# A hybrid decoder layer on one core: input-projection weights in sets of 256 columns, and the embedding weights kept on chip

## The chip, the cores and the metric

The kernel runs on one core of a Trainium2 chip. The core has five engines with queues of their own: TensorE (PE, with its weight loads shown as PEld), VectorE (DVE), ScalarE (ACT), GpSimd (POOL) and SyncE (SP), which here issues most of the DMAs. The metric is the device time of one execution in microseconds (us). Three runs of the kernel before took 2463.92 to 2465.51 us, with a median of 2464.99.

## What is computed

The reference is one decoder layer over 2048 tokens of width 1024, cut here to the parts that matter:

```python
u = rmsnorm(h, ln1_g)
q, k, v, g, g_lr, cb, cc, cx = split(u @ w_in)        # 256, 256, 512, 512, 16, 512, 512, 512 columns
log_a = log_sigmoid(g_lr @ w_gate_up + b_gate) / 16
o = gla_chunked(q / 8, k, v, log_a)                   # gated linear attention, 4 heads
o = rmsnorm(o, gn_g) * silu(g)
y = cb * causal_depthwise_conv(cc * cx, conv_w)
h = h + concat(o, y) @ w_out
a, b = split(rmsnorm(h, ln2_g) @ w_gate_upffn)        # 2 x 2816 columns
h = h + (silu(a) * b) @ w_down
gate = sigmoid(rmsnorm(h, ln3_g) @ w_ple_gate)
h = h + gate * (p @ w_ple_proj)                       # p: 2048 x 256 embeddings
return rmsnorm(h, lnf_g)
```

All data are float32.

## The kernel before

**Products.** Each float32 operand is split into a high part (the operand cast to fp32r) and a low part (the rest), by one cast on ScalarE and one subtraction on VectorE (`split`, lines 103 to 107, or `split_into`, line 161). `product` (line 144) multiplies, for each k of 128 rows, high by high, high by low and low by high: three matmuls per k. A `unit` (line 153) is such a product over the eight k of the width 1024, 24 matmuls of 128x512, followed by the eviction of its PSUM bank and by ticks. A tick advances delayed work and one step of the gated attention, which is written as a generator (`gla`, line 360) and so is interleaved with the units.

**Three phases.** The mixing phase does input projection, attention, convolution and output projection for four blocks of 512 tokens; at its end it turns the embeddings `p` of the first 1024 tokens and multiplies them by `w_ple_proj`. The up phase starts with the same product for the other 1024 tokens, and then multiplies by `w_gate_upffn` in seven products per group (a Strassen scheme, in the order 1, 6, 2, 5, 7, 3, 4), with operands U that the mixing phase has written to DRAM. The last phase does `w_down`, the gate and the final norm.

**Order of the queues.** In the mixing phase only PE's order is the program's; the other engines' queues are ordered at compile time by a scheduler. In the up and last phases all five queues follow the program. A queue runs strictly in its order, so an instruction that waits holds up all behind it.

**The input projection in a block** (`mixing`). First come v and the low-rank gate (528 columns). Then come five weight sets of 512 columns: `wq` (q and k), two `wc` (256 columns of cc with 256 of cx each), `wg` and `wb`. A set is loaded by `weights` (line 109) in four `raw` tiles of two k each, with rows of 2 KB (1 KB where the set has two segments), and split into eight `hl` tiles, one per k, each with 512 high and 512 low values per partition. Four units then read all eight tiles, each unit its own 128 columns. There are eleven `hl` buffers and four `raw` buffers, used in rotation. The weights are the stationary operand, the activations (`uT`) the moving one. The attention's generator starts with the first unit on `wq`; it puts chains on ScalarE, VectorE and GpSimd (`Abs`, `Exp`, `Ln`, a scan at line 378, then `level_elementwise`, lines 389 to 403).

**The embeddings.** `embedding_turned` (line 712) turns `p` on PE and, at the first call, loads and splits `w_ple_proj` into four `hl` tiles. `embedding` (line 719) multiplies. In the up phase (from line 862) `p` is loaded to two of the three `ur` buffers, `w_ple_proj` is loaded again to two `raw` buffers and split into a buffer of the pool `U2` (`wpp`), and `p` is turned and split into another (`p_turned`). Then come 16 units of six matmuls (u = 0 to 15). Between them, `events` fetch and cut the first operands U of the gate product: each fetch is two DMAs of 512 KB to `ur` buffers, each cut two casts and two subtractions. The operands of the first four products go to the pool `uT` (four buffers of 16 KB per partition, shared by both phases), the other three to `U2` (three buffers).

Of the kernel before, what the change touches and what calls it, by code (L numbers as in the profile page):

```python
# [8 lines left out]
F32 = mybir.dt.float32  # L9
# [5 lines left out]
P = 128  # L15
# [24 lines left out]
def hybrid_layer(ctx: ExitStack, tc: tile.TileContext,  # L40
# [68 lines left out]
    def weights(src, segs, k0=0, nk=NK, between=None):  # L109
        width = sum(n for _, n in segs)  # L110
        tiles = []
        for k in range(k0, k0 + nk, 2):
            raw = load_pair(src, k, width, segs)
            if between:
                between(k)
            for i in range(2):
                tiles.append(split(raw[:, i, :], width))
        return lambda k, s: tiles[k][:, s, :]

# [148 lines left out]
            split_into(dst(0, sl), dst(1, sl), tp)  # L270

    U = [{}, {}]

    def fetch_U(b, n, gate=None):

# [20 lines left out]
    def mixing_phase(st):  # L296
# [251 lines left out]
        def mixing(b, u1, first):  # L548

            vt = [w4([P, 2, 512]) for _ in range(2)]  # L550
            wv = weights(w_in, [(O_V, 512), (O_LR, 16)], between=first)

            def v_done(ps, ti, n):
                dst = vt[ti // 2][:, ti % 2, :]
                if n == 0:
                    nc.scalar.copy(out=dst[:, 0:264], in_=ps[:, 0:264])
                    return
                lr = tiny.tile([P, 16], F32, name="lr")
                nc.vector.tensor_copy(out=lr, in_=ps[:, 248:264])
                nc.scalar.copy(out=dst[:, 264:512], in_=ps[:, 0:248])  # L560

                def low_rank():
                    tp = tr_bank()
                    nc.tensor.transpose(out=tp[0:16, 0:P], in_=lr, identity=ident)
                    nc.vector.tensor_copy(out=lrT[0:16, ti * P:(ti + 1) * P], in_=tp[0:16, 0:P])
                later(2, low_rank)

            for ti in range(NT):
                if first is not None:
                    first(8 + ti)  # L570
                cols = [slice(n * 264, (n + 1) * 264) for n in range(2)]
                banks = [mm_bank() for _ in range(2)]
                lhs = uT_at(u1, tok_of(ti))
                if first is not None and ti == 0:
                    for k in range(NK):
                        for n in range(2):
                            for i, (a, c) in enumerate(PASSES):
                                nc.tensor.matmul(out=banks[n][:, 0:264], lhsT=lhs(k, a), rhs=wv(k, c)[:, cols[n]],
                                                 start=(k == 0 and i == 0), stop=(k == NK - 1 and i == 2))
                    v_done(banks[0], ti, 0)  # L580
                    v_done(banks[1], ti, 1)
                    continue
                for n in range(2):
                    unit(banks[n][:, 0:264], lhs, lambda k, s: wv(k, s)[:, cols[n]], NK,
                         lambda: v_done(banks[n], ti, n))
            mix = [None, None]
            wq = weights(w_in, [(O_Q, 512)])
            qT = w4([P, 2, T])
            kT = w4([P, 2, T])
            gsT = [w4([P, 2, T]) for _ in range(2)]  # L590
            side[0] = gla(qT, kT, vt, gsT, mix)
            for j in range(4):
                ps = mm_bank()

                def qk_done():
                    if j < 2:
                        nc.scalar.mul(out=qT[:, j, :], in_=ps, mul=0.125)
                    else:
                        nc.scalar.copy(out=kT[:, j - 2, :], in_=ps)
                unit(ps, lambda k, s: wq(k, s)[:, j * P:(j + 1) * P], uT_at(u1, full), NK, qk_done)  # L600

            mix[1] = big([P, 4, 2, T], F32R)
            yt = [w4([P, 2, T]) for _ in range(2)]
            for g in range(2):
                wc = weights(w_in, [(O_CC + g * 256, 256), (O_CX + g * 256, 256)])
                for jj in range(2):
                    j = g * 2 + jj
                    z = t2([P, T + 2])
                    pc = mm_bank()

                    def cc_done():
                        nc.gpsimd.tensor_copy(out=z[:, 0:2], in_=halo[:, j, :])
                        nc.scalar.copy(out=z[:, 2:T + 2], in_=pc)
                    unit(pc, lambda k, s: wc(k, s)[:, jj * P:(jj + 1) * P], uT_at(u1, full), NK, cc_done)
                    px = mm_bank()

                    def cx_done():
                        nc.vector.tensor_tensor(out=z[:, 2:T + 2], in0=px, in1=z[:, 2:T + 2], op=ALU.mult)
                        nc.gpsimd.tensor_copy(out=halo[:, j, :], in_=z[:, T:T + 2])
                        y = yt[g][:, jj, :]  # L620
                        nc.vector.tensor_scalar(out=y, in0=z[:, 2:T + 2], scalar1=cw[:, 2, j:j + 1], scalar2=None,
                                                op0=ALU.mult)
                        nc.vector.scalar_tensor_tensor(out=y, in0=z[:, 1:T + 1], scalar=cw[:, 1, j:j + 1], in1=y,
                                                       op0=ALU.mult, op1=ALU.add)
                        nc.vector.scalar_tensor_tensor(out=y, in0=z[:, 0:T], scalar=cw[:, 0, j:j + 1], in1=y,
                                                       op0=ALU.mult, op1=ALU.add)
                    unit(px, lambda k, s: wc(k, s)[:, 256 + jj * P:256 + (jj + 1) * P], uT_at(u1, full), NK, cx_done)
            wg = weights(w_in, [(O_G, 512)])
            for h in range(4):
                ps = mm_bank()  # L630

                def g_done():
                    gs = t2([P, T])
                    nc.scalar.activation(out=gs, in_=ps, func=AF.Silu)
                    nc.vector.tensor_scalar(out=gsT[h // 2][:, h % 2, :], in0=gs, scalar1=gng, scalar2=None, op0=ALU.mult)
                unit(ps, lambda k, s: wg(k, s)[:, h * P:(h + 1) * P], uT_at(u1, full), NK, g_done)

            wb = weights(w_in, [(O_CB, 512)])
            for j in range(4):
                ps = mm_bank()  # L640

                def cb_done():
                    y = yt[j // 2][:, j % 2, :]
                    last["cb"] = nc.vector.tensor_tensor(out=y, in0=ps, in1=y, op=ALU.mult)
                    split_into(mix[1][:, j, 0, :], mix[1][:, j, 1, :], y)
                unit(ps, lambda k, s: wb(k, s)[:, j * P:(j + 1) * P], uT_at(u1, full), NK, cb_done)
            while side[0] is not None:
                tick()
            return mix
# [62 lines left out]
        def embedding_turned(q):  # L712
# [1 line left out]
                emb0["pT"] = big([P, 4, 2, T], F32R)  # L714
            turned_p(emb0["p"][q], lambda s, sl: emb0["pT"][:, 2 * q:2 * q + 2, s, sl], tr_bank)
            if q == 0:
                emb0["w"] = [weights(w_pp, [(n * 512, 512)], 0, 2) for n in range(2)]

        def embedding():
            for ti in range(EQ * NT):  # L720
                o = w4([P, D])
                for n in range(2):
                    ps = mm_bank()
                    product(ps, lambda k, s: emb0["pT"][:, 2 * (ti // NT) + k, s, tok_of(ti % NT)], emb0["w"][n], 2)
                    nc.scalar.copy(out=o[:, n * 512:(n + 1) * 512], in_=ps)
                    tick()
                nc.gpsimd.dma_start(out=emb[ti], in_=o)
# [39 lines left out]
    def up_phase(st):  # L767
# [95 lines left out]
        for q in range(EQ, NB):  # L863
            pts.append(pl["ur"].tile([P, 2, T], F32, name="ur"))
            nc.sync.dma_start(out=pts[-1].rearrange("p a t -> p (a t)").rearrange("p (t d) -> p t d", t=NT),
                              in_=p[q * T:(q + 1) * T, :].rearrange("(t p) d -> p t d", p=P))
        wpp_raw = [raw().rearrange("p q n -> p (q n)").rearrange("p (k n) -> p k n", k=2) for _ in range(2)]
        for n in range(2):
            nc.sync.dma_start(out=wpp_raw[n], in_=w_pp[:, n * 512:(n + 1) * 512].rearrange("(k p) n -> p k n", p=P))
        p_turned, wpp = [pl["U2"].tile([P, 4, 2, T], F32R, name="U2") for _ in range(2)]  # L870
        for n in range(2):
            split_into(wpp[:, 2 * n:2 * n + 2, 0, :], wpp[:, 2 * n:2 * n + 2, 1, :], wpp_raw[n])

        def pT(q):
            return lambda k, s: p_turned[:, (q - EQ) * 2 + k, s, :]
        for q in range(EQ, NB):
            o = (q - EQ) * 2
            turned_p(pts[q - EQ].rearrange("p a t -> p (a t)").rearrange("p (t d) -> p t d", t=NT),
                     lambda s, sl: p_turned[:, o:o + 2, s, sl], mm_bank)
        cuts = []  # L880

        def fetch_next(j):
# [2 lines left out]
        def cut_all():  # L885
            while cuts:
                cuts.pop(0)()
        events = {0: lambda: (fetch_next(0), run(-6), run(-5), run(-4)), 3: lambda: (cut_all(), fetch_next(1)),
                  6: lambda: (cut_all(), fetch_next(2), run(-3)), 9: lambda: (cut_all(), fetch_next(3), run(-2)),
                  12: lambda: (cut_all(), fetch_next(4)), 13: lambda: run(-1)}  # L890
        stores = []
        u = 0
        for q in range(EQ, NB):
# [530 lines left out]
```

## Time and profile before

| what | value |
|---|---|
| median of three runs | 2464.99 us |
| the profiled execution | 2461.07 us |
| its span, first to last instruction | 2459.4 us |
| PE busy | 2373.1 us, 96% |
| DVE, ACT, POOL busy | 57%, 40%, 29% |
| mean granted clock of PE | 0.990 |
| mixing phase | about 0 to 947 us |
| up phase | about 947 to 1843 us |

In the page and its views, an engine's idle time stands before the instruction that ended it, with the one that released it behind an arrow (`<-`). `L148` is line 148 of the kernel; as helpers record the operations, one line serves many tiles, and the tiles' names tell them apart: `mm<-uT,hl` is the input projection from its second set on, `mm<-hl,uT` v, the output projection and the first embeddings' product, `mm<-U,U` the second phase's embeddings' product, `U<-raw` the split of `wpp`, `U<-mm` that of the turned `p`, `uT<-ur` and `U<-ur` the cuts of U. Matmuls overlap each other, so that one of 128x512 lasts about 390 ns in the records while a stream of them advances by about 224 ns each.

### The profile page before, as it was taken

To read this page: it belongs to the slowest core of one execution; us is meant where nothing else is said; L and a number is where in the kernel's file an instruction comes from. 1 tells how busy PE (TensorE), PEld (TensorE's weight loads), DVE (VectorE), ACT (ScalarE), POOL (GpSimd) and SP (SyncE) were. 2 spreads that over 40 slices of the span, in tenths; PEclk is the share of its full clock that TensorE was granted. 3 is DMA by queue.
4 is the path that set the end of the run, shared out by engine and by line. 5 is a ranking of instruction groups with operands and counts; after the bars stand their busy time and mean duration, and the time that the engine had idled before them with its cause. 6 is when DMAs were issued, how large, how long until landed. Compare 5 with 4: busy or idle time off the path is not lost. (4 is left out here: it accounts for less than half of the span.)

```text
span 2459.4 us, 31386 instructions
## 1 busy us (share of the span) xinstructions
PE 2373.1 (96%) x11752; PEld 1941.7 (79%) x11752; DVE 1397.8 (57%) x1676; ACT 975.6 (40%) x1533; POOL 705.7 (29%) x604
## 2 busy tenths in 40 slices
PE   7999999999999997999999999999999999999995
PEld 6777878777887786788888888888887888788774
DVE  4665475556646652655555655445546556655777
ACT  4434433453445334422222432222224344435556
POOL 3301210431103015334334244244532105301522
PEclk9999999999999998999999999999999999999998
DMA  4226322831442259735445675567757668866997
GB/s 156 69 69 202 109 85 102 247 110 57 170 158 69 69 175 293 280 135 185 150 155 171 208 270 202 193 216 255 257 204 288 201 226 282 284 194 227 322 330 287
DMA packets 274761, 471.08 MB, mean 192 GB/s; under 512 B 22688, under 2 KB 146096, under 8 KB 274608
## 3 DMA queue, kind: packets, MB, share of 16 engines
q1 hardware_dynamic: 272112, 460.66, 55.5%
q0 software_dynamic: 2496, 8.41, 1.4%
q8 instruction: 92, 1.51, 0.2%
q14 instruction: 61, 0.50, 0.1%
HBM read 326.92 MB, written 142.08 MB: 191 GB/s over the span
## 5 line engine op out<-in xcount | busy, mean ns | idle before, releaser
L1069 PE MATMUL ps<-wh,mh 128*128 128x512 f32 x2496 | 579.4, 393 | 11.7 <-ACT mh L162 6.3
L1069 PEld LDWEIGHTS ps<-wh,mh 128*128 128x128 f32 x2496 | 469.7, 189 | 115.1 <-ACT mh L162 9.1
L148 PE MATMUL mm<-uT,hl 128*128 128x512 f32 x1920 | 479.0, 403 | 9.8 <-DVE hl L106 6.0
L148 PE MATMUL mm<-uT,wu 128*128 128x512 f32 x2112 | 482.3, 389 | 0.0
L148 PEld LDWEIGHTS mm<-uT,wu 128*128 128x128 f32 x2112 | 396.6, 188 | 82.1
L148 PEld LDWEIGHTS mm<-uT,hl 128*128 128x128 f32 x1920 | 354.9, 189 | 103.6 <-DVE hl L106 11.4
L148 PE MATMUL mm<-U,wu 128*128 128x512 f32 x1584 | 362.9, 389 | 2.1 <-DVE v L218 2.1
L148 PEld LDWEIGHTS mm<-U,wu 128*128 128x128 f32 x1584 | 297.4, 188 | 64.0 <-issue 2.5
L163 DVE TENSOR_TENSOR wu<-raw,wu 128x1024 fp32r<-128x1024 f32 x154 | 221.7, 1440 | 205.8 <-ACT wu L162 205.8
L148 PE MATMUL mm<-hl,uT 128*128 128x512 f32 (+1 forms) x1584 | 299.1, 348 | 3.4 <-DVE uT L163 2.1
L148 PEld LDWEIGHTS mm<-hl,uT 128*128 128x128 f32 x1584 | 250.5, 189 | 42.7 <-DVE uT L163 2.7
L162 ACT CAST wu<-raw 128x1024 fp32r<-128x1024 f32 x154 | 161.4, 1049 | 302.6 <-PE mm L148 220.4
L163 DVE TENSOR_TENSOR wh<-wr,wh 128x1024 fp32r<-128x1024 f32 x111 | 141.2, 1272 | 219.9 <-ACT wh L162 219.5
L218 DVE TENSOR_TENSOR v<-mm,v 128x512 f32<-128x512 f32 x220 | 150.9, 687 | 149.8 <-PE mm L148 149.0
L218 POOL TENSOR_TENSOR v<-v,v 128x512 f32<-128x512 f32 x88 | 137.9, 1567 | 300.2 <-DMA hid<-v 234.3
L162 ACT CAST wh<-wr 128x1024 fp32r<-128x1024 f32 x111 | 110.8, 998 | 253.3 <-PE ps L1069 200.7
L106 DVE TENSOR_TENSOR hl<-raw,hl 128x512 fp32r<-128x512 f32 (+1 forms) x260 | 183.7, 744 | 27.5 <-ACT hl L105 27.2
L105 ACT CAST hl<-raw 128x512 fp32r<-128x512 f32 (+1 forms) x260 | 153.9, 623 | 62.7 <-PE mm L148 33.2
L218 POOL TENSOR_TENSOR raw<-raw 128x1024 f32<-128x1024 f32 x44 | 107.2, 2446 | 217.7 <-issue 154.7
L163 DVE TENSOR_TENSOR mh<-mr,mh 128x1024 fp32r<-128x1024 f32 x111 | 143.8, 1296 | 8.9 <-ACT mh L162 8.6
L162 ACT CAST mh<-mr 128x1024 fp32r<-128x1024 f32 x111 | 110.6, 997 | 12.7 <-DMA mr<-hid 7.7
L218 POOL TENSOR_TENSOR ur<-ur 128x512 f32<-128x512 f32 x60 | 95.2, 1587 | 32.0 <-DMA ur<-in_w_ple_gate_dram 26.9
(190 smaller groups left out, 1884.4 us busy)
## 6 DMA issues: line engine op xcount, KB each, us to landing
raw<-in_w_gate_upffn_dram SPq DMA_DIRECT2D x77, 512.0 KB, 4.5
hid<-v SPq DMA_DIRECT2D x154, 256.0 KB, 3.6
mr<-hid SPq DMA_DIRECT2D x70, 512.0 KB, 4.6
raw<-in_w_in_dram SPq DMA_DIRECT2D x64, 512.0 KB, 4.5
wu<-raw SPq DMA_DIRECT2D x44, 512.0 KB, 2.9
raw<-wu SPq DMA_DIRECT2D x44, 512.0 KB, 5.8
wr<-wd SPq DMA_DIRECT2D x40, 512.0 KB, 3.7
w<-in_x_dram SPq DMA_DIRECT2D x32, 512.0 KB, 8.9
```

Source lines behind the costliest of these rows:

```text
L105: nc.scalar.copy(out=hl[:, 0, :], in_=raw)
L106: nc.vector.tensor_tensor(out=hl[:, 1, :], in0=raw, in1=hl[:, 0, :].bitcast(F32), op=ALU.subtract)
L148: nc.tensor.matmul(out=out_ap, lhsT=lhs(k, a), rhs=rhs(k, b), start=(start and k == 0 and i == 0), stop=(k == nk - 1 and i == 2), **kw)
L162: nc.scalar.copy(out=hi, in_=src)
L163: nc.vector.tensor_tensor(out=lo, in0=src, in1=hi.bitcast(F32), op=ALU.subtract)
L218: return e.tensor_tensor(out=out, in0=a, in1=b, op=op)
L1069: nc.tensor.matmul(out=bk[n][t], lhsT=M[a][:, j, tok_of(t)], rhs=W[c][:, j, :], start=(on is None and k == 0 and i == 0), stop=(k == nk - ...
```

## The change

Two things change in the mixing phase and one in the up phase.

- A new helper `columns` loads 256 columns of all eight k: two `raw` tiles of four k each, rows of 1 KB (512 B where the set has two segments of 128), split into four `hl` tiles of two k each. Each old set of 512 becomes two, and each is requested just ahead of the two units that read it.
- `w_ple_proj` is split once, in the mixing phase, into a buffer of `uT` that both phases see (`shared["wpp"]`). The up phase neither loads nor splits it.
- As that buffer is taken until the second embeddings' product ends, the operand of the fourth product (n = 5, in `uT`) is fetched after that of the fifth (n = 7, in `U2`): `fetch_next(3)` and `fetch_next(4)` change places.

```diff
+    def columns(src, segs, nk=NK):
+        tiles = []
+        for k in range(0, nk, 4):
+            raw = pl["raw"].tile([P, 4, 256], F32, name="raw")
+            o = 0
+            for c, n in segs:
+                nc.sync.dma_start(out=raw[:, :, o:o + n],
+                                  in_=src[k * P:(k + 4) * P, c:c + n].rearrange("(k p) n -> p k n", p=P))
+                o += n
+            for i in range(0, 4, 2):
+                hl = pl["hl"].tile([P, 2, 2, 256], F32R, name="hl")
+                split_into(hl[:, 0], hl[:, 1], raw[:, i:i + 2, :])
+                tiles.append(hl)
+        return lambda k, s: tiles[k // 2][:, s, k % 2, :]
...
-            wq = weights(w_in, [(O_Q, 512)])
...
             for j in range(4):
                 ps = mm_bank()
+                if j % 2 == 0:
+                    wq = columns(w_in, [(O_Q + j * P, 256)])
...
-                unit(ps, lambda k, s: wq(k, s)[:, j * P:(j + 1) * P], uT_at(u1, full), NK, qk_done)
+                unit(ps, lambda k, s: wq(k, s)[:, tok_of(j % 2)], uT_at(u1, full), NK, qk_done)
...
-                wc = weights(w_in, [(O_CC + g * 256, 256), (O_CX + g * 256, 256)])
                 for jj in range(2):
                     j = g * 2 + jj
+                    wc = columns(w_in, [(O_CC + j * P, P), (O_CX + j * P, P)])
...
             if q == 0:
-                emb0["w"] = [weights(w_pp, [(n * 512, 512)], 0, 2) for n in range(2)]
+                shared["wpp"] = big([P, 4, 2, T], F32R)
+                for n in range(2):
+                    raw = load_pair(w_pp, 0, 512, [(n * 512, 512)])
+                    for k in range(2):
+                        split_into(shared["wpp"][:, 2 * n + k, 0, :], shared["wpp"][:, 2 * n + k, 1, :], raw[:, k, 0:512])
...
-        wpp_raw = [raw().rearrange("p q n -> p (q n)").rearrange("p (k n) -> p k n", k=2) for _ in range(2)]
-        for n in range(2):
-            nc.sync.dma_start(out=wpp_raw[n], in_=w_pp[:, n * 512:(n + 1) * 512].rearrange("(k p) n -> p k n", p=P))
-        p_turned, wpp = [pl["U2"].tile([P, 4, 2, T], F32R, name="U2") for _ in range(2)]
-        for n in range(2):
-            split_into(wpp[:, 2 * n:2 * n + 2, 0, :], wpp[:, 2 * n:2 * n + 2, 1, :], wpp_raw[n])
+        p_turned, wpp = pl["U2"].tile([P, 4, 2, T], F32R, name="U2"), shared["wpp"]
...
-                  6: lambda: (cut_all(), fetch_next(2), run(-3)), 9: lambda: (cut_all(), fetch_next(3), run(-2)),
-                  12: lambda: (cut_all(), fetch_next(4)), 13: lambda: run(-1)}
+                  6: lambda: (cut_all(), fetch_next(2), run(-3)), 9: lambda: (cut_all(), fetch_next(4), run(-2)),
+                  12: lambda: (cut_all(), fetch_next(3)), 13: lambda: run(-1)}
```

`wg` and `wb` are edited as `wq` is, and the two embeddings' products read `shared["wpp"]`.

More of the change, by code (lines that the diff above doesn't have):

```diff
@@ L272, in hybrid_layer @@
     U = [{}, {}]
+    shared = {}
     def fetch_U(b, n, gate=None):
@@ L613, in cc_done @@
                         nc.scalar.copy(out=z[:, 2:T + 2], in_=pc)
-                    unit(pc, lambda k, s: wc(k, s)[:, jj * P:(jj + 1) * P], uT_at(u1, full), NK, cc_done)
+                    unit(pc, lambda k, s: wc(k, s)[:, 0:P], uT_at(u1, full), NK, cc_done)
                     px = mm_bank()
@@ L626, in cx_done @@
                                                        op0=ALU.mult, op1=ALU.add)
-                    unit(px, lambda k, s: wc(k, s)[:, 256 + jj * P:256 + (jj + 1) * P], uT_at(u1, full), NK, cx_done)
-            wg = weights(w_in, [(O_G, 512)])
+                    unit(px, lambda k, s: wc(k, s)[:, P:2 * P], uT_at(u1, full), NK, cx_done)
             for h in range(4):
                 ps = mm_bank()
+                if h % 2 == 0:
+                    wg = columns(w_in, [(O_G + h * P, 256)])
                 def g_done():
@@ L635, in g_done @@
                     nc.vector.tensor_scalar(out=gsT[h // 2][:, h % 2, :], in0=gs, scalar1=gng, scalar2=None, op0=ALU.mult)
-                unit(ps, lambda k, s: wg(k, s)[:, h * P:(h + 1) * P], uT_at(u1, full), NK, g_done)
-            wb = weights(w_in, [(O_CB, 512)])
+                unit(ps, lambda k, s: wg(k, s)[:, tok_of(h % 2)], uT_at(u1, full), NK, g_done)
             for j in range(4):
                 ps = mm_bank()
+                if j % 2 == 0:
+                    wb = columns(w_in, [(O_CB + j * P, 256)])
                 def cb_done():
@@ L645, in cb_done @@
                     split_into(mix[1][:, j, 0, :], mix[1][:, j, 1, :], y)
-                unit(ps, lambda k, s: wb(k, s)[:, j * P:(j + 1) * P], uT_at(u1, full), NK, cb_done)
+                unit(ps, lambda k, s: wb(k, s)[:, tok_of(j % 2)], uT_at(u1, full), NK, cb_done)
             while side[0] is not None:
@@ L723, in embedding @@
                     ps = mm_bank()
-                    product(ps, lambda k, s: emb0["pT"][:, 2 * (ti // NT) + k, s, tok_of(ti % NT)], emb0["w"][n], 2)
+                    product(ps, lambda k, s: emb0["pT"][:, 2 * (ti // NT) + k, s, tok_of(ti % NT)],
+                            lambda k, s: shared["wpp"][:, 2 * n + k, s, :], 2)
                     nc.scalar.copy(out=o[:, n * 512:(n + 1) * 512], in_=ps)
```

## The prediction

> **What bounds the kernel now.** I read the page first, then the waits of TensorE, then the timeline and the table of windows around each wait that the change can reach.
>
> ```profile
> span 2459.4 us, 31386 instructions
> ...
> PE 2373.1 (96%) x11752; PEld 1941.7 (79%) x11752; DVE 1397.8 (57%) x1676; ACT 975.6 (40%) x1533; POOL 705.7 (29%) x604
> ```
>
> TensorE (PE) is busy for 2373.1 of 2459.4 us, and the change takes no matrix product away. It can therefore win only PE's idle time, 86 us in all (that is 2459.4 - 2373.1), and time at a reduced clock. The waits of PE say who ends its idle time:
>
> ```profile
> PE mm L148 <- ACT U L162: 13.0, 1, 13.0
> ...
> PE mm L148 <- DVE hl L106: 6.0, 8, 1.2
> ...
> PE mm L148 <- ACT hl L105: 3.7, 4, 2.2
> ```
>
> The columns are the total, the number of waits and the longest. The first is a single wait of 13 us. The other two, 9.7 us together, are waits for split weights (`hl`) of the input projection. Those are the two places that the change touches; the lines left out lie at the kernel's start, at transposes and in the last phase.
>
> **The input projection.** The waits for `hl` are not spread over the sets. All of them lie at one place in each of the four blocks, the start of the third weight set (the first `wc`). The table of windows over those four places (after the length of the window comes PE's busy time, and after the counts of the five engines PE's granted clock and the DMA share), and a narrower one of the second place:
>
> ```profile
> 71.00:83.00 12.00, 9.27 (x37) 6.44 (x36) 9.85 (x15) 7.80 (x13) 3.49 (x3) 1.00 0.50 148
> 296.00:308.00 12.00, 9.85 (x34) 6.51 (x33) 10.68 (x12) 9.46 (x15) 7.61 (x6) 0.86 0.37 105
> 525.00:537.00 12.00, 9.84 (x34) 6.57 (x33) 10.90 (x12) 9.25 (x15) 7.40 (x6) 0.86 0.38 105
> 752.00:764.00 12.00, 9.23 (x37) 6.29 (x36) 10.81 (x12) 9.31 (x15) 7.50 (x6) 1.00 0.37 103
> ```
> ```profile
> 302.00:306.00 4.00, 3.52 (x8) 2.27 (x8) 4.00 (x6) 3.20 (x6) 1.61 (x2) 0.59 0.59 164
> ```
>
> PE is idle there for 2.7, 2.2, 2.2 and 2.8 us, 9.8 in all. In the second and third block the clock drops as well: 0.59 over 4 us loses 4 x 0.41 = 1.6 us, 3.3 for both. So 13.1 us lie here. The timeline of the second block shows the cause:
>
> ```profile
> 293.51 0.21 ACT L387 ACTIVATE ebl<-w 128x8 f32<-128x8 f32 x1 [3.55 <-DVE w L378]
> ...
> 297.68 1.06 ACT L401 ACTIVATE uT<-uT 128x1024 f32<-128x1024 f32 x1 [0.50 <-POOL uT L400]
> 298.65 2.68 ACT L105 CAST hl<-raw 128x512 fp32r<-128x512 f32 x5
> ...
> 299.30 0.74 PE L148 MATMUL mm<-uT,hl 128*128 128x512 f32 x2 [0.50 <-ACT hl L105]
> ```
>
> ScalarE (ACT) has waited in its queue on the gated attention's own chain of VectorE and GpSimd; the five casts stand behind that and start at 298.65, when PE already needs the first of them.
>
> How much delay can be borne follows from the eleven `hl` buffers. A matmul of 512 columns takes 0.224 us at full clock (the 968 to 987 row below: 18.60 us for 83), a unit of 24 takes 5.4. Before, a set is eight tiles, each holding one k, and each is read in all four units. The buffer of its first tile comes free three matmuls (0.7 us) into the last unit, and takes the next set's fourth tile, which is needed three tiles (2.0 us) into the next unit: 5.4 + 2.0 - 0.7 = 6.7 us later. After, a set is four tiles of two k each, read in two units. Its first tile is free 6 x 0.224 = 1.3 us into the second unit and takes the fourth tile of the set after the next: 5.4 + 10.8 + 4.0 - 1.3 = 18.9 us. In the example the buffer was free about 0.7 us into the unit that began near 291 us, so the cast came some 7 us late. That breaks a slack of 6.7 us, less a cast and a subtraction; it leaves 12 of 18.9. A set's start also needs four casts where it needed eight, one for each 1.3 us of PE's work.
>
> ```profile
> L106 DVE TENSOR_TENSOR hl<-raw,hl 128x512 fp32r<-128x512 f32 x228 | 159.0, 735 | 18.9 <-ACT hl L105 18.7
> L105 ACT CAST hl<-raw 128x512 fp32r<-128x512 f32 x228 | 134.5, 621 | 58.0 <-PE mm L148 33.2 <-DMA raw<-in_w_in_dram 10.0 <-DMA raw<-in_w_out_dram 7.0
> ```
>
> The count and size of these instructions do not change (160 casts and 160 subtractions of 128x512 over the five old sets of four blocks, as many over the ten new ones). Nor does PE's order of matmuls. The loads, casts and subtractions of a second half are now written behind the first half's two units and the attention's steps among them, so they are moved past those on SP, ACT and VectorE; no instruction of GpSimd is moved. The lower bound of the gain is what remains if the casts stay behind the attention's chain: the first tile still costs the 0.50 and about 1.2 us of VectorE's wait, then the slower demand ends the stall. That would keep some 1.7 x 4 = 6.8 of the 9.8 us and win 3. The upper bound is 13.1. I take 10: the slack speaks for nearly all of it, but the order of ACT's queue here is the scheduler's, and twenty more set starts give it new places to be late.
>
> Costed at nothing: the loads. As many bytes come in as many DMAs, but in rows of 1 KB where they were 2 KB, and of 512 B where they were 1 KB.
>
> ```profile
> raw<-in_w_in_dram SPq DMA_DIRECT2D x64, 512.0 KB, 4.5
> raw<-in_w_in_dram SPq DMA_DIRECT2D x64, 256.0 KB, 4.0
> ```
> ```profile
> 272.00:410.00 138.00, 135.84 (x806) 105.28 (x805) 86.44 (x133) 58.09 (x122) 28.83 (x29) 0.99 0.25 77
> ```
>
> Half the bytes in rows half as long took 4.0 us against 4.5, so a byte cost 1.8 times as much. Doubled everywhere, the DMA share of 0.25 becomes 0.5, and a landing 8 to 9 us. The cover is that idle half and the raw buffers, which are loaded ahead of the casts. With the cover gone, 4 us per set would show, at most 160 us; nothing in this window comes near that.
>
> **The hand-over at 949 us.** The timeline, from the last embeddings of the first phase to the first product of the second, without the small rows:
>
> ```profile
> 944.90 2.34 SPq L869 DMA_DIRECT2D raw<-in_w_ple_proj_dram  x2
> ...
> 947.43 1.91 PE L267 MATMUL mm<-ident,ur 128*128 128x128 f32 x16
> 947.63 0.58 ACT L725 COPY w<-mm 128x512 f32<-128x512 f32 x1 [0.82 <-PE mm L148]
> ...
> 959.46 1.04 ACT L162 CAST U<-raw 128x1024 fp32r<-128x1024 f32 x1 [11.24 <-DMA raw<-in_w_ple_proj_dram]
> ...
> 961.74 2.04 ACT L162 CAST U<-mm 128x512 fp32r<-128x512 f32 x4
> 962.37 0.50 PEld L148 LDWEIGHTS mm<-U,U 128*128 128x128 f32 x2 [13.27 <-ACT U L162]
> ```
> ```profile
> 955.00:962.00 7.00, 0.00 (x0) 0.00 (x0) 1.36 (x2) 2.26 (x3) 0.00 (x0) 0.50 1.03 389
> 962.00:968.40 6.40, 5.88 (x13) 4.20 (x14) 3.48 (x5) 2.36 (x5) 1.78 (x1) 0.50 0.98 320
> 968.40:987.00 18.60, 18.60 (x83) 15.39 (x83) 11.71 (x8) 13.24 (x19) 6.34 (x3) 1.00 0.75 234
> ```
>
> PE has turned `p` by 949.3 and then waits for `wpp`, whose two loads are issued at 944.90 into full queues (share 1.03) and have come only at 959.46; the casts of the turned `p` stand behind them in ACT's queue. The change removes both loads (2.34 us of SP, ahead of the loads of U), two casts and two subtractions. What is late next is the first cast of the turned `p`: ACT is free at 948.2, the cast takes 2.04 / 4 = 0.5 us, so it is ready about when the transposes end, and PE goes on near 949.4. That wins 13.0 us. The clock of 0.50 from 962 to 968.4 cost 6.4 x 0.5 = 3.2 us after the gap and goes with it: 16.2 us.
>
> The Trainium skill, "TensorE: Matmul & The Clock Gate", Part 1: The HAM clock gate, says that the clock falls to half after an idle window of about 3.4 us. The hand-over agrees. The input projection does not: no wait for `hl` is over 2.2 us (last column of the waits), and the clock fell in the two blocks with less idle time. By the page those 3.3 us would not belong to the waits and the sum would be 3.3 smaller; I go by the rows.
>
> Not all of the 16.2 stays won, because the second phase's operands come through the same full queues. The first cut of U (n = 1) stands at the fourth unit of the embeddings' product, three units in; two `ur` buffers hold `p`, so n = 6 can be loaded only as the cuts free them. This is a cast of the second of them, and the landing time of such loads in this stage:
>
> ```profile
> 977.43 1.05 ACT L162 CAST uT<-ur 128x1024 fp32r<-128x1024 f32 x1 [1.97 <-DMA ur<-up]
> ```
> ```profile
> ur<-up SPq DMA_DIRECT2D x14, 512.0 KB, 6.9
> ```
>
> After the change n = 1 takes `wpp`'s place in the queue and can be cut from 959.5 on. Its buffer frees near 962, n = 6 lands 6.9 us later, at 969, and ACT has two casts of it and one of the first up weights (1.05 each) ahead of the eviction of unit 6. That eviction then comes at 972. Units last 6 x 0.224 = 1.34 us; with eight PSUM banks unit 14 needs unit 6's bank, and would start at 949.4 + 14 x 1.34 = 968.2. So PE, which now waits for nothing there, waits about 4 us, perhaps with another 1.6 of clock. The later cuts (n = 2, 7, 5) run by the same chain while PE stands nearer to it, and n = 5, used fourth, is now fetched fifth, because `wpp` keeps its `uT` buffer; that leaves one product (24 x 0.224 = 5.4 us) less of slack. I put 0 to 4 us on these, and take 6 for all that is given back. The bounds are 0, and the case in which the DMAs alone set this stage. Then only the bytes removed count, 1.05 MB at 389 GB/s = 2.7 us, and the lull that can be filled:
>
> ```profile
> 970.00:975.00 5.00, 5.00 (x24) 4.14 (x23) 3.59 (x2) 4.37 (x7) 5.00 (x2) 1.00 0.21 66
> ```
>
> That is 5 x 0.79 = 4.0 us; so 6.7 us of the 16.2 would stay, or 2.7 if the lull stays too. I take 16.2 - 6 = 10.
>
> The first phase's side costs nothing: four casts and four subtractions of `wpp` are written to a `uT` buffer instead of four `hl` tiles; that buffer held the attention's scratch, done long before. If it were late, the first product of the embeddings would wait for a cast and a subtraction, 1.4 us. `hl` comes free earlier.
>
> **The sum.** 10 + 10 = 20 us. The profiled execution took 2461.07 us (span and 1.67 around it), so a like one would take 2441; the median of the runs, 2464.99, stands 3.9 above it, so I forecast 2445.
>
> **The rivals.** (a) The input projection's stalls stay, since ACT's order puts the new casts behind the same chain. The bounds above leave 3 + 10: 2452. For it speaks that all four blocks stall at the same set, so that the attention's chain and not chance makes the delay; against it, the slack of 18.9 us. (b) The hand-over is bound by its DMAs: 10 + 2.7 to 6.7, which is 2448 to 2452. The share of 1.03 speaks for it, the lull against. Both together give 3 + 2.7: 2459. (c) Slower: the second half of each old set is now requested after the first half's units, so if ACT's queue follows that order, the casts come behind the eviction of the unit just before their use. Then each of 40 set starts shows a cast and a subtraction, 0.62 + 0.74 plus two hand-overs, about 1.6 us: 64 us lost against 20 won, some 2509. It begins to lose from 13 such starts on. Against it: before, the sets stand behind the last set's evictions in the same way, and sixteen of twenty starts show no wait. (d) The change doesn't do what it says for `wpp`: the turned `p` is held by memory that the first phase still uses, until its stores of embeddings are through, and PE resumes no earlier than about 959. Then the hand-over wins 3, for 2452. By the sizes of the pools that buffer lies over `hl` and `raw`, which are done; so this is unlikely.
>
> **How the numbers follow.** My forecast (both parts win, within 6 us of 2445) has 0.58, (a) 0.12, (b) with (d) 0.17, both parts small 0.08, (c) 0.05. All gains whole, 13.1 + 16.2, would give 2436; the range goes from there to 2457, which takes in (a), (b) and (d) and leaves out (c) and the worst of both. A measurement of this kernel tells about 0.2% (4.9 us) from no change, so same is 2460 to 2470: faster 0.87, same 0.08, slower 0.05.
>
> **What would show it.** Right: the 13 us wait of PE on ACT at line 162 gone, no loads of `w_ple_proj` in the second phase, its first product less than 1 us after the transposes, a new wait of some us about 20 us later that ends with an eviction, and the waits for `hl` below 3 us with the clock at 1.00 there. Wrong: waits for `hl` at the starts of second halves (c), the same waits at the third old set (a), or PE's time from the first embeddings' product of the second phase to the first gate product longer by 8 us or more than its 16 x 1.34 = 21.4 (b).

## The result, and the profile after

| | before | changed |
|---|---|---|
| median beside each other | 2465.25 us (2463.92 to 2466.33, 4 runs) | 2439.98 us (2437.46 to 2443.70, 4 runs) |
| ratio, 95% interval | | 0.990, 0.9887 to 0.9913 |
| profiled execution | 2461.07 us | 2438.52 us |

The change wins 25.3 us by the medians and 22.6 us in the profiled pair (spans of 2459.4 and 2436.8 us). The forecast was 2445, with a range of 2436 to 2457. A second measurement of the changed kernel, `after_again`, on another occasion gave 2441.32 us and a ratio of 0.9895 (0.988 to 0.991).

The waits of TensorE in the changed kernel, with the columns as before (total, number, longest):

```profile
PE tr L219 <- DVE w L212: 10.3, 1, 10.3
...
PE mm L164 <- DVE v L234: 4.1, 1, 4.1
PE mm L164 <- ACT v L921: 2.3, 1, 2.3
```

The 13.0 us for `U` and all waits for `hl` have gone from the list. Two waits take their place: a new one of 2.3 us for an eviction (`v`, L921), and one of 4.1 us for VectorE, which was 2.1 us before. The table of windows over the input projection of the second, third and fourth block of the changed kernel (length, PE's busy time, ..., PE's granted clock, DMA share, GB/s):

```profile
258.00:395.00 137.00, 137.00 (x854) 109.59 (x853) 85.53 (x129) 59.38 (x120) 30.34 (x27) 1.00 0.27 78
486.00:625.00 139.00, 139.00 (x863) 111.08 (x861) 89.27 (x135) 61.34 (x123) 31.20 (x28) 1.00 0.32 93
715.00:853.00 138.00, 138.00 (x839) 108.88 (x839) 92.70 (x141) 62.37 (x130) 31.55 (x29) 1.00 0.28 85
```

PE has no idle time there and the clock is whole. The DMA share is 0.27 to 0.32 where it was 0.24 to 0.25, and most of the rise is bytes: in the third block, 93 GB/s pass where it was 76. So shorter rows cost almost nothing of the queues. The DMA issues of the changed kernel say the same (size of one, median us to landing):

```profile
raw<-in_w_in_dram SPq DMA_DIRECT2D x64, 512.0 KB, 3.8
raw<-in_w_in_dram SPq DMA_DIRECT2D x64, 256.0 KB, 3.9
```

The landings took 4.5 and 4.0 us before; 256 KB now take as long as 512 KB, so the time was not a price per byte. The timeline of ScalarE in the second block shows the cause of the stalls still in place, and passed by:

```profile
276.44 0.62 ACT L178 CAST hl<-raw 128x512 fp32r<-128x512 f32 x1 [0.86 <-PE mm L164]
277.83 0.62 ACT L178 CAST hl<-raw 128x512 fp32r<-128x512 f32 x1 [0.77 <-PE mm L164]
...
285.32 1.12 ACT L178 CAST hl<-raw 128x512 fp32r<-128x512 f32 x2
...
290.73 0.21 ACT L404 ACTIVATE ebl<-w 128x8 f32<-128x8 f32 x1 [2.98 <-DVE w L395]
293.24 1.06 ACT L418 ACTIVATE uT<-uT 128x1024 f32<-128x1024 f32 x1 [2.29 <-POOL uT L417]
```

The attention's chain (L404, L418) still waits in ScalarE's queue. But the four casts of the first set of `wc` stand ahead of it. The last two are done at 286.4 us, and PE starts on that set at about 293.3. The casts of the second set of `wc` do stand among and behind the chain; the last of them ends at 303.3 us, ahead of PE's start on that set at 304.5.

The hand-over between the phases in the changed kernel, from the timeline:

```profile
932.92 1.91 PE L283 MATMUL mm<-ident,ur 128*128 128x128 f32 x16
933.11 0.59 ACT L750 COPY w<-mm 128x512 f32<-128x512 f32 x1 [0.77 <-PE mm L164]
933.60 2.06 ACT L178 CAST U<-mm 128x512 fp32r<-128x512 f32 x4
...
934.36 8.49 SPq L815 DMA_DIRECT2D raw<-in_w_gate_upffn_dram  x4
...
934.58 19.33 PE L164 MATMUL mm<-uT,U 128*128 128x512 f32 x84
...
952.45 1.05 ACT L178 CAST uT<-ur 128x1024 fp32r<-128x1024 f32 x1 [5.64 <-DMA ur<-up]
...
953.71 1.04 ACT L178 CAST uT<-ur 128x1024 fp32r<-128x1024 f32 x1 [0.21 <-DMA ur<-up]
954.66 1.04 ACT L178 CAST wu<-raw 128x1024 fp32r<-128x1024 f32 x1
955.61 1.55 ACT L921 COPY v<-mm 128x512 f32<-128x512 f32 x3
...
956.24 1.22 PE L164 MATMUL mm<-uT,U 128*128 128x512 f32 x2 [2.33 <-ACT v L921]
```

PE goes on with the product at 934.58 us, when its transposes end. No load or split of `w_ple_proj` is left; SP issues the gate product's weights instead. Fourteen units later (84 matmuls) PE needs a PSUM bank, whose eviction stands behind two cuts and a cast of weights in ScalarE's queue. The first of those cuts had waited 5.64 us for its load of U. The table of windows for that wait, and for twice 3.4 us behind it:

```profile
953.90:956.20 2.30, 0.01 (x1) 0.00 (x0) 2.30 (x1) 2.30 (x4) 1.50 (x1) 1.00 0.55 222
956.20:959.60 3.40, 3.36 (x8) 2.72 (x9) 3.40 (x4) 1.90 (x3) 0.00 (x0) 0.50 0.59 134
959.60:963.00 3.40, 3.40 (x16) 2.78 (x16) 1.14 (x2) 1.92 (x3) 0.00 (x0) 1.00 1.04 336
```

At half clock the first 3.4 us lose another 1.7. The wait of 4.1 us for VectorE ends a chain of the same kind, 37 us later:

```profile
981.54 1.05 ACT L178 CAST U<-ur 128x1024 fp32r<-128x1024 f32 x1 [5.97 <-DMA ur<-up]
...
988.16 1.22 DVE L179 TENSOR_TENSOR U<-ur,U 128x1024 fp32r<-128x1024 f32 x1 [1.44 <-ACT U L178]
...
992.26 1.28 DVE L234 TENSOR_TENSOR v<-mm,v 128x512 f32<-128x512 f32 x2
993.09 12.08 PE L164 MATMUL mm<-U,wu 128*128 128x512 f32 x45 [4.14 <-DVE v L234]
```

The eviction (`v`, L234) stands behind two cuts of U and a subtraction of weights in VectorE's queue, and ScalarE's casts for those cuts had waited for loads of U.

**Where the time came from.** PE's order of matmuls is the same in both traces, so the lead of the changed kernel can be read from the starts of the same matmul:

| place | before | changed | lead |
|---|---|---|---|
| 90 matmuls around each block's third set, four blocks | 24.73, 25.69, 25.65, 24.82 us | 21.00 us each | +16.9 in all |
| first transpose of `p`, second phase | 947.43 | 932.92 | 14.5 |
| 16 matmuls into the embeddings' product | 969.19 | 938.33 | 30.9 |
| 8 matmuls after the wait for VectorE in the gate product | 1018.71 | 996.09 | 22.6 |
| span | 2459.4 | 2436.8 | 22.6 |

The input projection wins 16.9 us, of which 2.4 are lost again ahead of the hand-over, mostly to new spells of half clock (last section). The hand-over wins 16.4 us and gives back 8.3 within 60 us.

### The profile page after: what moved, and what is told of

Its sections match the earlier page's. It is cut to its first block, busy times and chain, and to the rows that moved or that the text cites. A ratio compares the mean times of both kernels' runs of the same rounds, so it can differ in the third digit from the quotient of the medians.

```text
span 2436.8 us, 31370 instructions
## 1 busy us (share of the span) xinstructions
PE 2366.4 (97%) x11752; PEld 1940.5 (80%) x11752; DVE 1401.1 (57%) x1674; ACT 972.9 (40%) x1531; POOL 713.7 (29%) x604
## 4 chain that ended last, share of the span: by engine, by line
PE 67%; DMA 5%; DVE 3%; issue 2%; ACT 2%; POOL 1%; SPq 1%; POOLq 0%; DVEq 0%; ACTq 0%
PE mm L164 48%; PE ps L1090 16%; DMA mr<-hid 1%; DMA ur<-up 1%; PE g L444 1%; DVE mh L179 1%; DMA pp<-emb 1%; DMA wr<-wp 1%; POOL as L234 1%; DMA mr<-u 1%; DMA out_dram<-w 1%; DVE h L234 0%; DMA wr<-in_w_ple_gate_dram 0%; PE ps L1123 0%; SPq L815 0%
## 5 line engine op out<-in xcount | busy, mean ns | idle before, releaser
L1090 PE MATMUL ps<-wh,mh 128*128 128x512 f32 x2496 | 578.0, 392 | 13.1 <-ACT mh L178 7.5
L164 PE MATMUL mm<-uT,hl 128*128 128x512 f32 x1920 | 472.1, 400 | 0.0
L164 PE MATMUL mm<-hl,uT 128*128 128x512 f32 (+1 forms) x1488 | 278.6, 346 | 3.4 <-DVE uT L179 2.1
L164 PEld LDWEIGHTS mm<-hl,uT 128*128 128x128 f32 x1488 | 234.8, 190 | 39.1 <-DVE uT L179 2.7
L234 DVE TENSOR_TENSOR v<-mm,v 128x512 f32<-128x512 f32 x220 | 151.0, 688 | 154.9 <-PE mm L164 154.0
L234 POOL TENSOR_TENSOR v<-v,v 128x512 f32<-128x512 f32 x88 | 140.8, 1600 | 301.3 <-DMA hid<-v 285.4
L234 POOL TENSOR_TENSOR raw<-raw 128x1024 f32<-128x1024 f32 x44 | 106.0, 2419 | 210.5 <-issue 152.7
L179 DVE TENSOR_TENSOR hl<-raw,hl 128x512 fp32r<-128x512 f32 x160 | 118.6, 765 | 49.2 <-ACT hl L178 49.0
L178 ACT CAST hl<-raw 128x512 fp32r<-128x512 f32 x160 | 93.8, 618 | 73.9 <-PE mm L164 62.5
L234 POOL TENSOR_TENSOR ur<-ur 128x512 f32<-128x512 f32 x60 | 93.2, 1553 | 31.3 <-DMA ur<-in_w_ple_gate_dram 27.9
```

Of the source, the lines that this page charges most:

```text
L164: nc.tensor.matmul(out=out_ap, lhsT=lhs(k, a), rhs=rhs(k, b), start=(start and k == 0 and i == 0), stop=(k == nk - 1 and i == 2), **kw)
L178: nc.scalar.copy(out=hi, in_=src)
L179: nc.vector.tensor_tensor(out=lo, in0=src, in1=hi.bitcast(F32), op=ALU.subtract)
L234: return e.tensor_tensor(out=out, in0=a, in1=b, op=op)
L1090: nc.tensor.matmul(out=bk[n][t], lhsT=M[a][:, j, tok_of(t)], rhs=W[c][:, j, :], start=(on is None and k == 0 and i == 0), stop=(k == nk - ...
```

## The experiments

Each ratio is to the kernel before, measured beside it, with its 95% interval.

**The two halves of the change, alone.** In `columns_only` the new column sets stand, and `wpp` is loaded and split in both phases as before. In `wpp_only` the old sets stand and `wpp` is kept.

```diff
 # columns_only, against the changed kernel
-                shared["wpp"] = big([P, 4, 2, T], F32R)
-                ...
+                emb0["w"] = [weights(w_pp, [(n * 512, 512)], 0, 2) for n in range(2)]
```

> The sets of 256 columns alone; the embeddings' weights are loaded and split in both phases, as before. If the two parts are independent, this keeps the lead that PE has in the changed kernel before the hand-over, 14 us, and the hand-over waits 13 us as before: 2449 to 2453 us, no waits for hl in the input projection. If most of the gain comes from the hand-over, or if the sets of 256 need the hl buffers that the embeddings' weights no longer take, waits for hl remain and it is above 2456.

> The kept embeddings' weights alone (with the changed order of fetches); the input projection in sets of 512 as before. If the parts are independent: the 13 us wait gone, the waits for hl as before (9.7 us in twelve waits), and of the 16.7 us won at the hand-over some 9 given back later: 2456 to 2460 us. If the give-back belongs to the hand-over being early in time or to the new sets, and not to the fetches, nothing is given back: about 2449.

`columns_only` took 2448.63 us, 0.9932 (0.9915 to 0.9949); `wpp_only` 2459.62 us, 0.9978 (0.9969 to 0.9988). Against their 2465.8 us of the kernel before these are gains of 17.2 and 6.2 us. Their sum of 23.4 is the whole of 25.3 within the spread of the runs, so the halves add. The waits of `columns_only`:

```profile
PE mm L164 <- ACT U L178: 13.2, 1, 13.2
```

The wait of the hand-over is whole, and there is none for `hl`. The waits of `wpp_only` show the reverse:

```profile
PE mm L148 <- DVE hl L106: 5.4, 7, 1.2
PE mm L148 <- DVE v L218: 4.6, 1, 4.6
PE mm L148 <- ACT v L901: 4.2, 2, 2.6
PE mm L148 <- ACT hl L105: 3.7, 4, 2.2
```

It also shows that the give-back belongs to the kept `wpp` with its changed order of fetches: 2.6 us on an eviction (the longest of L901) and 4.6 on VectorE (L218).

**Is the slack of the buffers what the columns bring?** First try, `hold6`: six of eleven `hl` buffers were to be held while the third set came in.

```diff
+            held = [pl["hl"].tile([P, 2, 2, 256], F32, name="hl") for _ in range(6)]
+            for t in held:
+                nc.gpsimd.memset(t[:, 0, 0, 0:1], 0.0)
...
+            for t in held:
+                nc.gpsimd.tensor_copy(out=t[:, 0, 0, 1:2], in_=t[:, 0, 0, 0:1])
```

> The changed kernel with six of the eleven hl buffers held idle from the first wc set to the end of the input projection of each block, so that sets of four tiles have five buffers: a buffer freed in a set's second unit is needed again about 5.4 us later, less than the 6.7 of before. If slack of buffers is what ended the stalls, waits for hl come back at the start of the first wc set, 1 to 2.5 us in each block, and the time is 2444 to 2450. If the halved number of casts per set is what ended them, there are none and it stays at 2440.

It took 2443.97 us, 0.9917 (0.9902 to 0.9932), with no wait for `hl`, and tells nothing about slack. Nothing tied the release to the work, so the queue of GpSimd let each buffer go at once:

```profile
272.50 0.10 POOL L624 MEMSET hl<- 128x1 f32 x1 [21.32 <-PE mm L164]
272.66 0.59 POOL L671 COPY hl<-hl 128x1 f32<-128x1 f32 x1
```

It serves as a control, since it has all the added instructions. In `hold6_to_end` and `hold3_to_end` the release reads a result of the block's last unit:

```diff
-                nc.gpsimd.tensor_copy(out=t[:, 0, 0, 1:2], in_=t[:, 0, 0, 0:1])
+                nc.gpsimd.tensor_copy(out=t[:, 0, 0, 0:1], in_=yt[1][:, 1, 0:1])
```

> The changed kernel with six of the eleven hl buffers held from the first sets of a block to its last unit of the input projection, the release tied to that unit's result. Sets of four tiles then have five buffers. If slack of buffers is what ended the stalls, the casts of the first wc set must again wait for the unit just before, stand behind the attention's chain in ScalarE's queue, and PE waits for hl there, 1 to 3 us in each block; other set starts may wait too: 2445 to 2460 us. If sets of four tiles suffice by themselves, no waits and 2440 to 2444.

> The changed kernel with three of the eleven hl buffers held from the request of the first set of wc until the end of the block's input projection, so that sets of 256 columns turn over in eight. With eight buffers of two k each, the buffer of a set's first tile was freed 4.1 us into the last unit of the set before the last and is needed after two more units and what is left of that one: 1.3 + 10.8 = 12.1 us at the least over the four tiles, against 4.4 to 6.7 with five buffers and a lateness of about 7 us. Theory (slack in buffers is what the narrower sets bring): no wait for hl, 2440 to 2445 us. Rival (the stall with six held came from the holding instructions or from any loss of buffers): waits for hl again, about half as many as with six held, 2450 to 2460.

With six held: 2464.71 us, 0.9996 (0.9986 to 1.0005). With three held: 2440.78 us, 0.989 (0.9876 to 0.9905). Waits of the kernel with six held:

```profile
PE mm L164 <- ACT hl L178: 9.9, 4, 4.9
...
PE mm L164 <- DVE hl L179: 4.2, 4, 1.2
```

These stalls lie at the old place, the first set of `wc`, and the timeline of ScalarE there has the old cause:

```profile
299.05 0.21 ACT L404 ACTIVATE ebl<-w 128x8 f32<-128x8 f32 x1 [3.49 <-DVE w L395]
301.18 1.06 ACT L418 ACTIVATE uT<-uT 128x1024 f32<-128x1024 f32 x1 [1.92 <-POOL uT L417]
...
303.22 1.06 ACT L418 ACTIVATE uT<-uT 128x1024 f32<-128x1024 f32 x1 [0.51 <-POOL uT L417]
304.19 0.60 ACT L178 CAST hl<-raw 128x512 fp32r<-128x512 f32 x1
```

The slack, counted as in the prediction, is 5.4 us with five buffers free (a set's second tile takes the buffer of the first tile of the set just before) and 5.4 - 1.3 + 10.8 = 14.9 us with eight; the figures in the expectation, 4.4 to 6.7 and 12.1, were counted too low. The casts come some 7 us late. A slack of 5.4 or 6.7 breaks, and with 5.4 the stalls cost 20.7 us, most of what the change wins: 2464.71 against 2443.97 for the same instructions without the hold. 14.9 holds as well as 18.9. The idle time goes the same way: 1.3 us less slack than before the change, and 14.1 us of waits in four blocks against 9.7, which is 1.1 us more in each. Sets of four tiles alone do not do it, since the kernel with six held has them too. (These slacks are counted with the prediction's 0.224 us for each matmul. By their starts the matmuls of the input projection advance by 0.233 us, 21.00 us for 90. The 0.224 is low in part because the 83 of the prediction's window include those that its edges cut: by the starts in that window it is 0.227. With 0.233 the slacks are 5.6, 7.0, 15.4 and 19.6 us, and the order stays.)

**Is the attention's chain what makes the casts late?** `chain_late` is the kernel before with the first chain requested six ticks later:

```diff
-            yield
-            yield
+            for _ in range(8):
+                yield
...
-GLA_WAIT = 10
+GLA_WAIT = 4
```

> The kernel before, with the attention's first chain (Abs, Exp, Ln, scan) six ticks later and the wait after it six ticks shorter, so that ScalarE has no wait on that chain ahead of the first wc set. If that chain in ScalarE's queue makes the stall, the twelve waits for hl at the first wc set go or move to a later set start, with 2452 to 2462 us if they go. If eight casts per set or late loads make it, they stay at 9.7 us at that place and the time is 2465.

It took 2494.82 us, 1.0121 (1.0106 to 1.0136). The chain is the cause, since no wait for `hl` is left, with the same sets and buffers as before. But the price is larger than the stalls, and my expected time was wrong. What follows the chain becomes late instead: PE waits in the attention's own products (`g`) for ScalarE and VectorE:

```profile
PE g L417 <- ACT s_sb L421: 28.8, 12, 5.6
...
PE g L417 <- DVE uT L403: 4.6, 3, 1.5
```

**What takes back half of the hand-over's gain?** By one theory it is the order of ScalarE's queue: the eviction that PE needs stands behind a cut. By the rival the transfers set the pace of this stage. Four kernels change the order or the buffers. `p_in_raw` loads `p` to two `raw` buffers, so that all three `ur` serve U. `cuts_later` moves the events of the second phase by two units. `cuts_only_later` moves only the cuts and fetches. `later_and_stores` also issues ten of the sixteen stores of embeddings one by one beside the gate products. A fifth, `no_stores`, has no such stores in this stage.

```diff
 # cuts_only_later
-                  6: lambda: (cut_all(), fetch_next(2), run(-3)), 9: lambda: (cut_all(), fetch_next(4), run(-2)),
-                  12: lambda: (cut_all(), fetch_next(3)), 13: lambda: run(-1)}
+                  6: lambda: run(-3), 8: lambda: (cut_all(), fetch_next(2)), 9: lambda: run(-2),
+                  11: lambda: (cut_all(), fetch_next(4)), 13: lambda: run(-1),
+                  14: lambda: (cut_all(), fetch_next(3))}
```

> The changed kernel with the second phase's p loaded to two raw buffers (those that the embeddings' weights had) instead of two of the three ur buffers, so that the loads of U need not wait for p to be turned or cut. If the want of ur buffers delays the second operand (n = 6), its cut comes some 5 us earlier and the 2.3 us wait for unit 6's eviction goes, with the clock's drop after it: 2434 to 2437. If the full DMA queues delay it, the wait stays at about 2 us and the time at 2440.

> The changed kernel with the cuts of the second, third and fourth operand at units 8, 11 and 14 instead of 6, 9 and 12, so that two more evictions stand ahead of each in ScalarE's queue. If the wait of 2.3 us is the order of that queue, it goes; the operands come a little later, which may show as waits before the gate product's first products of 0 to 3 us: 2435 to 2441. If the operands' DMAs set the pace, what is won at unit 14 comes back within the next 30 us and the time is 2440 or above.

> The changed kernel with the cuts and loads of U in the embeddings' product of the second phase two units later (8, 11, 14 for 6, 9, 12), while the weights' steps stay at 6, 9 and 13. Theory (the cut of n = 6 ahead of an eviction costs 2.3 us of wait and 1.7 of half clock): that wait is gone, no wait for wu as where both were moved, 2436 us. Rival (the transfers set this stage, so that a wait only changes its place): a wait for U or for a VectorE eviction grows by as much, 2440.

> As the kernel before, and ten of the sixteen stores of embeddings of the second phase are issued one by one beside the gate products, after the loads of U. Theory (the stores stand ahead of loads in SP's queue and take their bandwidth; without any of them the last wait of 4.1 us fell to 0.9): 2433 to 2436. Rival (the same bytes have to pass in the same 50 us): 2438 to 2442, the wait for the VectorE eviction stays at 3 to 5 us.

> The changed kernel without the sixteen stores of the second phase's embeddings (4 MB); in their place tiles of x are stored early in the first block, so that the last phase reads rows that are not the embeddings. If the DMA traffic after the hand-over causes what is given back there, the waits of 2.3 and 4.1 us shrink to under 3 us together and PE keeps at least 4 us more of its lead. If the order of the queues or the number of ur buffers causes it, both waits stay as they are.

The last column is PE's time from its last 16 transposes of `p` to its first matmul after the wait for VectorE, the stage's length.

| kernel | median us | ratio | stage, us |
|---|---|---|---|
| before | 2465.25 | | 69.4 |
| changed | 2439.98 | 0.990 (0.9887 to 0.9913) | 60.2 |
| `p_in_raw` | 2446.29 | 0.9921 (0.9904 to 0.9937) | 54.9, behind a wait of 11.3 |
| `cuts_later` | 2441.95 | 0.9898 (0.9883 to 0.9913) | 59.8 |
| `cuts_only_later` | 2439.78 | 0.9886 (0.9869 to 0.9902) | 60.8 |
| `later_and_stores` | 2439.75 | 0.9888 (0.9874 to 0.9903) | 59.6 |
| `no_stores` | 2435.93, one run | | 55.6 |

In `cuts_only_later` the wait for the eviction went, as meant. The timeline of its PE shows that another took its place:

```profile
935.88 22.04 PE L164 MATMUL mm<-uT,U 128*128 128x512 f32 x96
957.75 11.04 PE L164 MATMUL mm<-uT,wu 128*128 128x512 f32 x48
974.65 12.70 PE L164 MATMUL mm<-uT,wu 128*128 128x512 f32 x48 [5.86 <-ACT v L957]
987.19 5.60 PE L164 MATMUL mm<-U,wu 128*128 128x512 f32 x24
995.05 10.22 PE L164 MATMUL mm<-U,wu 128*128 128x512 f32 x37 [2.26 <-DVE v L234]
```

All 96 matmuls of the embeddings' product run through, and PE stops 5.86 us in the gate product instead. Three other orders (`cuts_later`, `cuts_only_later`, `later_and_stores`) give 59.6 to 60.8 us against 60.2, so the order of cuts, evictions and stores is not what sets this stage. The theory that I had put first falls. The windows over this stage of the changed kernel and of `no_stores`:

```profile
932.92:993.10 60.18, 53.43 (x234) 43.09 (x232) 32.21 (x29) 34.45 (x47) 11.06 (x6) 0.97 0.97 338
```
```profile
937.65:993.20 55.55, 52.84 (x233) 43.21 (x232) 32.51 (x29) 34.13 (x47) 12.48 (x6) 0.97 0.83 289
```

The changed kernel's transfers have a mean share of 0.97, with a lull of 0.55 to 0.59 from 953.9 to 959.6. With the stores away the share is 0.83, the stage is 4.6 us shorter, and PE's waits in it fall to 1.9 and 0.9 us. So the bytes of the stage cost time here, though PE's own 53 us stand close behind. `no_stores` stores other tiles to those places at the kernel's start, and comes 4.7 us later to these transposes (937.65 against 932.92); so its total time understates what the stores cost here. `p_in_raw` had the stage itself down to 54.9 us, but its loads of `p` were issued only at 931.10, took 14.0 us in the full queues, and PE waited 11.3 us for them, in which the other loads went on. It keeps all the stores, gives U a third `ur` buffer, and has fewer bytes left to move in the stage (326 GB/s over 54.87 us, 17.9 MB, against 20.3). So the runs do not part the bytes from a want of `ur` buffers, which the lull points to: around its start SP waits 4.0 us for a cut to free one. That both PE waits end chains of late loads of U is shown; what makes those loads late is shown in part. None of the variants is faster than the changed kernel by more than the spread of their runs.

## Why the prediction was right, step by step

- **The input projection: right, and mis-sized.** The term was 10 us, with 13.1 as the upper bound. It measured 16.9 in the blocks and 14.5 of lead at the hand-over. The bound was too low because it added PE's idle time as the records show it. A matmul's record lasts about 396 ns there, where the stream advances by 233, so each wait begins to be counted some 0.16 us after PE has fallen behind; twelve waits make 2.0 us. By the starts in the trace, the matmul behind a wait also takes about 0.34 us to the next start instead of 0.23, which makes some 1.4 more over all of them. The other 0.4 of 16.9 - 13.1 can't be assigned. The 3 us taken off for "new places to be late" were not needed: none of the new set starts shows a wait.
- **The slack argument: right.** 6.7 us broke and 18.9 held, and with held buffers 5.4 broke and 14.9 held, so the limit lies between 6.7 and 14.9 us. One picture was off: the casts of the first set of `wc` do not come late with slack to spare, they come ahead of the chain, 7 us before PE needs them.
- **The loads at nothing: right.** The share rose by at most 0.07, not by 0.25 as the landing times had suggested, and landings were not longer. The reading that a byte in half as long a row costs 1.8 times as much was wrong.
- **The hand-over's gain: right.** 16.2 us predicted, 16.4 measured; the first product began as the transposes ended.
- **The give-back: the mechanism in part, the size too small.** The term was 6 us: 4 for the eviction behind the cut of n = 6 at unit 14, perhaps 1.6 of clock, and 0 to 4 for later cuts. At unit 14, where it was predicted, came 2.33 us, and 1.7 of clock with it; later came 2.0 more for VectorE (4.1 against 2.1) and some 1.3 of clock behind that; small differences make up the 8.3. The step that failed is the reading of the queue's order as what sets the price: with that wait taken away in `cuts_only_later`, one of 5.86 us came in its place. Rival (b), the transfers, came nearer, though by the mark set for it the stage stood well: from the first embeddings' product to the first gate product 26.1 us (934.58 to 960.65), where 29.4 would have spoken for (b). Its gain of 2.7 to 6.7 us was too small (16.4 - 8.3 = 8.1 stayed), because it took the lull that can be filled from one window of 5 us. Up to 0.8 us before its end, the stage of the kernel before moved 318 GB/s in 68.6 us, 21.8 MB, and the changed one's whole stage 338 GB/s in 60.2 us, 20.3 MB. An estimate from these: 21.8 MB at 338 GB/s would take 64.5 us, so of the shorter stage some 4 us go with fewer bytes and as many with fuller queues. The windows of before over that stage:

```profile
947.43:1016.00 68.57, 54.08 (x233) 43.85 (x231) 34.61 (x30) 36.58 (x49) 11.48 (x6) 0.90 0.92 318
```

- **The sum.** 10 + 10 were predicted; 14.5 + 8.1 = 22.6 came in the profiled pair. That the sum is so near has luck in it: the first term was 4.5 too small and the second 1.9 too large. The medians' 25.3 us differs from 22.6 by less than the changed kernel's runs spread (2437.46 to 2443.70).
- **The rivals.** (a) and (c) are refuted by the waits: no start of a set shows one for `hl`. (d) is refuted by the product's start at 934.58.

## What to carry to other kernels

When an engine waits for operands that another engine prepares, count for how long a buffer lies free before its contents are needed, and compare that with the longest hold in the preparing engine's queue: cutting a set in two can raise the slack without a byte of memory more, and beyond the hold more slack brings nothing (here 14.9 us did as well as 18.9, against a hold of about 7). Before a gap is booked as gain, look at the DMA share of the whole stretch in which the following operands come: in this stage, with 0.92 before the change, half of the gap closed at its head opened again further on, and moving cuts, evictions and stores about only moved it. The idle time in TensorE's records was a lower bound of what its waits cost: 9.8 us of it, and 3.3 of lost clock, stood for 16.9.

## What the runs showed of the hardware

PE's clock fell to half behind waits much shorter than the one at the hand-over. In the changed kernel's output projection of the second block, by the timeline of PE:

```profile
447.10 1.04 PE L219 MATMUL tr<-ident,w 128*128 128x128 f32 x8
449.35 0.65 PE L219 MATMUL tr<-ident,w 128*128 128x128 f32 x4 [1.21 <-DVE uT L179]
450.97 1.10 PE L219 MATMUL tr<-ident,w 128*128 128x128 f32 x4 [0.97 <-ACT w L250]
```

and by the windows:

```profile
448.00:456.00 8.00, 5.82 (x23) 4.60 (x22) 4.28 (x5) 3.02 (x6) 5.22 (x6) 0.79 0.81 239
```

Two waits of 1.21 and 0.97 us within 3 us lowered the mean clock to 0.79 over 8 us, about 1.7 us lost. The Trainium skill, "TensorE: Matmul & The Clock Gate", Part 1: The HAM clock gate, has the clock fall after an idle window of about 3.4 us, and come back after a busy one of that length. At this place no idle time of 3.4 us occurs; what agrees is the length of a spell, 0.50 over the 3.40 us from 956.2 and 1.00 over the next. The measured rows decide: two short waits close together were enough here, though in the third block waits of 1.30 and 0.95 us in the same place drew no such spell. The runs do not show what decides between the two; a spell moves an execution by about 1.7 us.
